# Attention inside a gated decoder block: compressed blocks padded to full tiles, and a head's scaling, transposes and products issued in other steps

## Chip, cores and metric

The program runs on one core of one Trainium2 chip. The metric is device time of one execution in microseconds (us). The engines are named as in the profile: PE is TensorE's matmul side and PEld its weight load, DVE is VectorE, ACT is ScalarE, POOL is GpSimd, SP is the queue that issues most DMAs. Each engine takes its instructions in program order.

## Reference, cut to what matters

One decoder layer in float32 over 256 tokens and 2048 channels. The part that the change touches is the attention of 16 heads of 128 channels in 4 key/value groups. At 256 tokens every selected block is selected and the window covers everything, so a head has three softmaxes over the same queries:

```python
s_c = q . kc          # 15 compressed blocks (padded to 16), masked by block end
s_s = q . k_sel       # 256 keys, causal
s_w = q . k_win       # 256 keys, causal
o = gate0 * softmax(s_c) @ vc + gate1 * softmax(s_s) @ v_sel + gate2 * softmax(s_w) @ v_win
y = sig(gA) * o + sig(gB) * GLU(S5(u))
```

Around it stand large products with weights from HBM: the GLU product `y_s @ w_glu`, the output product, and the MLP.

## The kernel before

All large products are split in two: a weight tile `raw` (128x1024) is rounded on ACT into `hi` (L117), DVE subtracts it into `lo` (L120), and PE multiplies hi by hi, hi by lo and lo by hi (L316, L318, L319). One such tile is a *matmul unit*: 24 matmuls of 256 columns. `run_units` writes out a hand-made order: for each unit it issues the rounding on ACT, then the PE batch of the unit two before it, then the subtraction on DVE, then the steps of background generators that are due. So the instructions of a step stand on DVE behind this unit's `lo`, on ACT behind its `hi`, and on PE behind the batch.

The GLU stage has 32 matmul units, m0 to m31 here. After each of m10 to m25 come two *ada units*, whose second one issues 32 passes with a 32-column weight into the PSUM bank T3 (L1072, about 1.0 us on PE), after which ACT copies 128 columns out of T3 into `s`. Every fourth such pair is followed, after the next batch, by four transposes of `s` into T3 (L1081), which DVE reduces. When a pass of 8 units ends (its last batch runs at m9, m17 and m25), ACT applies four tanh (L1347) and DVE four products ahead of that unit's `lo`.

The attention is a background generator of 34 steps. Its planner gives at matmul unit m5+j, with j from 0 to 25, the steps up to ceil(34*(j+1)/26); nothing is due at ada units. With head h, step 2h is: scores(h) on PE (3 products, banks T0 and T12), the transposes of head h-1 (turn1 into T3, turn2 into A2, with ACT copies to SBUF), and exps(h) (masks and maxima on DVE, six exponentials on ACT). Step 2h+1 is weigh(h) (sums, reciprocal, gates and scaling: nine DVE operations, two ACT copies at L1269) and values(h-1) (five products into A3, L1296 to L1300, and one DVE product). The steps fall so: m5 has 0 and 1, m6 2, m7 3, m8 4 and 5, m9 6, m10 7, m11 8 and 9, m12 10, m13 11, m14 12 and 13, and so on; m25 has 27, m26 28, m27 29 and 30, m28 31, m29 32, m30 33. T0, T12, T3, A2, A3 exist once each: a writer waits until the last reader of the bank's previous use is done. The `hi` and `lo` tiles have three buffers, `P` and `sm` two.

Of the kernel before, what the change touches and what calls it, by code (L numbers as in the profile page):

```python
# [18 lines left out]
NH = 16  # L19
# [12 lines left out]
ATTN_WAIT = 5  # L32
# [49 lines left out]
def block_kernel(ctx, tc, cst_in, x, c, w_ada, b_ada, g_mix, w_in, w_ck2, pe_ck,  # L82
# [3 lines left out]
    nc = tc.nc  # L86
    V, A, PE = nc.vector, nc.scalar, nc.tensor
# [28 lines left out]
    def copy(out, in_, scale=1.0):  # L116
        A.activation(out=out, in_=in_, func=AF.Copy, scale=scale)  # L117
# [19 lines left out]
    ident = cst[:, 0:128]  # L137
# [39 lines left out]
    d_vc = scratch("d_vc", [32, 512])  # L177
# [8 lines left out]
    marks = {}  # L186
# [906 lines left out]
    at = {}  # L1093

    def attn_setup():
        r = region("RX", 16384)
        at["r"] = r
        at["q"] = r[:, 0:4096].rearrange("p (h t) -> p h t", h=16)
        at["v"] = r[:, 4096:6144].rearrange("p (t s n) -> p t s n", t=2, s=2)
        at["K"] = r[:, 6144:8256].rearrange("p (g n) -> p g n", g=4)  # L1100
        at["m"] = r[:, 8256:12352].rearrange("p (h t) -> p h t", h=16)
        at["free"] = r[:, 12352:16384]
        for i, n in enumerate(("tA", "tB")):
            at[n] = region(f"RB{i}", 4096).rearrange("p (h t) -> p h t", h=16)
        nc.sync.dma_start(out=at["K"][:, :, 0:16], in_=d_kc.rearrange("p (g n) -> p g n", g=4))
        vc = cp.tile([128, 512], FT, tag="k0", name="vc")
        nc.sync.dma_start(out=vc[0:32], in_=d_vc)
        at["vc"] = vc.rearrange("p (g n) -> p g n", g=4)
        for g in range(4):
            hs_ = slice(4 * g, 4 * g + 4)  # L1110
            nc.sync.dma_start(out=at["q"][:, hs_, :], in_=d_q[:, hs_, :])
            for s in range(2):
                nc.sync.dma_start(
                    out=at["K"][:, g, 16:528].rearrange("p (t s n) -> p t s n", t=2, s=2)[:, :, s, :],
                    in_=d_k[:, 4 * s + g, :].rearrange("p (t n) -> p t n", t=2))
            yield
            nc.sync.dma_start(out=at["v"][:, :, :, 128 * g:128 * g + 128], in_=d_v[:, :, :, 128 * g:128 * g + 128])
            nc.sync.dma_start(out=at["tA"][:, hs_, :], in_=d_g[:, hs_, :])
            yield
            yield  # L1120
# [91 lines left out]

    def attention():
        fa = at["free"]
        P = [fa[:, 832 * i:832 * i + 832] for i in range(2)]
        PT = [fa[:, 1664:2688]] * 2
        sm = [fa[:, 2688 + 32 * i:2720 + 32 * i] for i in range(2)]
        for i in range(2):
            V.memset(P[i][:, 768:832], 0.0)
        q, K, vv, m = at["q"], at["K"], at["v"], at["m"]  # L1220

        S = {}
# [9 lines left out]
        def exps(h):  # L1232
            S0, S1 = S["s"]
            p, s_ = P[h % 2], sm[h % 2]
            mx, nm, su, mb = s_[:, 0:6], s_[:, 6:12], s_[:, 12:18], s_[:, 18:20]
            pc = p[:, 768:832].rearrange("p (i n) -> p i n", i=2)
            tt(S0[:, 0:272], S0[:, 0:272], m0, OP.add)
            V.tensor_reduce(out=mx[:, 0:1], in_=S0[:, 0:16], axis=AX.X, op=OP.max)
            V.tensor_reduce(out=mx[:, 1:3], in_=S0[:, 16:272].rearrange("p (s n) -> p s n", s=2), axis=AX.X, op=OP.max)
            tt(S1[:, 0, 0:16], S1[:, 0, 0:16], m1c, OP.add)  # L1240
            ts(nm[:, 0:3], mx[:, 0:3], -1.0, OP.mult)
            tt(S1[:, 1, 16:272], S1[:, 1, 16:272], m0[:, 16:272], OP.add)
            V.tensor_reduce(out=mx[:, 3:4], in_=S1[:, 0, 0:16], axis=AX.X, op=OP.max)
            V.tensor_reduce(out=mx[:, 4:6], in_=S1[:, :, 16:272].rearrange("p b (s n) -> p s b n", s=2), axis=AX.XY, op=OP.max)
            ts(nm[:, 3:6], mx[:, 3:6], -1.0, OP.mult)
            A.activation(out=pc[:, 0, 0:16], in_=S0[:, 0:16], func=AF.Exp, bias=nm[:, 0:1])
            for s in range(2):
                A.activation(out=p[:, 128 * s:128 * s + 128], in_=S0[:, 16 + 128 * s:144 + 128 * s], func=AF.Exp,
                             bias=nm[:, 1 + s:2 + s], accum_out=su[:, 1 + s:2 + s])
            A.activation(out=pc[:, 1, 0:16], in_=S1[:, 0, 0:16], func=AF.Exp, bias=nm[:, 3:4])  # L1250
            for s in range(2):
                A.activation(out=p[:, 256 + 256 * s:512 + 256 * s].rearrange("p (b n) -> p b n", b=2),
                             in_=S1[:, :, 16 + 128 * s:144 + 128 * s], func=AF.Exp,
                             bias=nm[:, 4 + s:5 + s], accum_out=su[:, 4 + s:5 + s])

        def weigh(h):
            p, s_ = P[h % 2], sm[h % 2]
            su, cf = s_[:, 12:18], s_[:, 20:26]
            pc = p[:, 768:832].rearrange("p (i n) -> p i n", i=2)
            tt(pc[:, :, 0:16], pc[:, :, 0:16], okm, OP.mult)  # L1260
            V.tensor_reduce(out=su.rearrange("p (i b) -> p i b", i=2)[:, :, 0], in_=pc[:, :, 0:16], axis=AX.X, op=OP.add)
            ts(su, su, 1e-30, OP.max)
            V.reciprocal(out=cf, in_=su)
            tt(cf.rearrange("p (i b) -> p i b", i=2), cf.rearrange("p (i b) -> p i b", i=2),
               gates[:, :, 3 * h:3 * h + 3], OP.mult)
            for i in range(2):
                ts(pc[:, i, 0:16], pc[:, i, 0:16], cf[:, 3 * i:3 * i + 1], OP.mult)
            for s in range(2):
                A.activation(out=p[:, 128 * s:128 * s + 128], in_=p[:, 128 * s:128 * s + 128], func=AF.Copy,  # L1269
                             scale=cf[:, 1 + s:2 + s])  # L1270
                ts(p[:, 256 + 256 * s:512 + 256 * s], p[:, 256 + 256 * s:512 + 256 * s], cf[:, 4 + s:5 + s], OP.mult)

        def turn1(h):
            p, o = P[h % 2], PT[h % 2]
            ps = bank("T3")
            for s in range(2):
                PE.transpose(ps[:, 256 * s:256 * s + 128], p[:, 128 * s:128 * s + 128], ident)
                PE.transpose(ps[:, 256 * s + 128:256 * s + 256], p[:, 256 + 256 * s:384 + 256 * s], ident)
            copy(o[:, 0:512], ps)

        def turn2(h):
            p, o = P[h % 2], PT[h % 2]
            ps = bank("A2")
            for s in range(2):
                PE.transpose(ps[:, 128 * s:128 * s + 128], p[:, 384 + 256 * s:512 + 256 * s], ident)
            for i in range(2):
                PE.transpose(ps[0:32, 256 + 128 * i:384 + 128 * i], p[:, 768 + 32 * i:800 + 32 * i], ident)
            copy(o[:, 512:768], ps[:, 0:256])
            copy(o[0:32, 768:1024], ps[0:32, 256:512])

        def values(h):
            g = h // 4
            o = PT[h % 2]
            ps = bank("A3")
            hd = slice(128 * g, 128 * g + 128)
            PE.matmul(out=ps[:, 0:256], lhsT=vv[:, 0, 0, hd], rhs=o[:, 0:256], start=True, stop=False, skip_group_check=True)  # L1296
            PE.matmul(out=ps[:, 0:256], lhsT=vv[:, 0, 1, hd], rhs=o[:, 256:512], start=False, stop=False, skip_group_check=True)
            PE.matmul(out=ps[:, 0:256], lhsT=at["vc"][0:32, g, :], rhs=o[0:32, 768:1024], start=False, stop=False, skip_group_check=True)
            PE.matmul(out=ps[:, 128:256], lhsT=vv[:, 1, 0, hd], rhs=o[:, 512:640], start=False, stop=False, skip_group_check=True)
            PE.matmul(out=ps[:, 128:256], lhsT=vv[:, 1, 1, hd], rhs=o[:, 640:768], start=False, stop=True, skip_group_check=True)  # L1300
            stt(m[:, h, :], at["tA"][:, h, :], 1.0, ps[:, 0:256], OP.add, OP.mult)

        for h in range(NH + 1):
            if h < NH:
                scores(h)
            if h:
                turn1(h - 1)
                turn2(h - 1)
            if h < NH:
                exps(h)  # L1310
            yield
            if h < NH:
                weigh(h)
            if h:
                values(h - 1)
            yield


# [320 lines left out]
    with tc.manual_schedule():  # L1639
# [39 lines left out]
        def at_(name, f, nxt):  # L1679
# [18 lines left out]
            dict(name="load", gen=attn_setup(), start=marks["glu"] + AS0, end=marks["glu"] + AS1, total=13),  # L1698
            dict(name="tb", gen=load_tb(), start=marks["glu"] + TB0, end=marks["glu"] + TB1, total=4, tick=True),
            dict(name="ht", gen=h_tokens(), start=marks["down"] + 6, end=marks["down"] + 46, total=8),  # L1700
            dict(name="attn", gen=attention(), start=marks["glu"] + ATTN_WAIT, end=marks["out"] - 2, total=34),
        ]
        run_units(bgs)

# [46 lines left out]
```

## Time and profile before

| what | value |
|---|---|
| runs shown | 1748.01 us median of 3 (1745.74 to 1749.41) |
| profiled execution | 1746.7 us, of which 1744.9 us are the span of the profile |
| granted clock, mean over the span | 0.989 |
| PE, DVE, ACT busy over the span | 96%, 67%, 49% |
| attention, first scores to last values | 719.14 to 891.52 us from the span's start |

The profile shows one execution. Busy shares are averages over stages; what the change can be worth is read from the stretch of the attention alone. A group in brackets at a row's end is the idle time of that engine just ahead of it and what ended it.

### The profile page before, as it was taken

What the parts mean: (1) busy time and instruction counts of PE and PEld (TensorE: products, weight loads), DVE (VectorE), ACT (ScalarE), POOL (GpSimd) and SP (SyncE); (2) the same over time, 40 slices, a digit from 0 to 9 for tenths busy, and PEclk for the clock granted to TensorE, in tenths of its full rate; (3) what the DMA queues carried; (4) which work ended last, traced back from release to release, by engine and by line L of the source; (5) the groups of instructions that cost most, each with busy time, mean ns of one, the idle gap of its engine ahead of it and who ended that gap; (6) DMA issues with size and microseconds to landing.
All of it is one profiled execution on the core that took longest, in us unless ns stands there. A gap on an engine that the chain in (4) does not pass through costs nothing.

```text
span 1744.9 us, 31373 instructions
## 1 busy us (share of the span) xinstructions
PE 1682.4 (96%) x12478; PEld 1443.4 (83%) x12478; DVE 1166.3 (67%) x2168; ACT 858.8 (49%) x1424; POOL 30.6 (2%) x53
## 2 busy tenths in 40 slices
PE   6999999889999999999999999999999999999997
PEld 4788899778888877878889999888888888887885
DVE  4868567438898987666656676666666655566555
ACT  3443443564444468655554454444444455555554
POOL 1000000210000000000000000000000000000000
PEclk8999999999999999999999999999999999999999
DMA  8988755948878867966658747777777565655662
GB/s 329 347 274 313 257 182 193 295 137 298 301 266 283 255 220 249 307 233 224 212 184 293 261 156 231 232 241 238 241 249 237 191 189 188 192 190 186 193 194 91
DMA packets 148691, 407.97 MB, mean 234 GB/s; under 512 B 13936, under 2 KB 18512, under 8 KB 147520
## 3 DMA queue, kind: packets, MB, share of 16 engines
q1 hardware_dynamic: 141680, 386.54, 67.3%
q0 software_dynamic: 2032, 10.72, 1.7%
q10 hardware_dynamic: 4832, 8.70, 1.4%
q8 instruction: 98, 1.61, 0.4%
q14 instruction: 49, 0.40, 0.1%
HBM read 386.93 MB, written 16.88 MB: 231 GB/s over the span
## 4 chain that ended last, share of the span: by engine, by line
PE 84%; DVE 7%; ACT 5%; DMA 2%; issue 1%; SPq 0%; ACTq 0%; DVEq 0%
PE A L344 21%; PE A L345 11%; PE A L316 7%; PE A L1615 6%; PE A L318 6%; PE A L1613 6%; PE A L1614 6%; PE A L319 6%; DVE lo L120 3%; PE T L1072 2%; PE T L368 2%; ACT hi L117 1%; ACT RX L117 1%; DMA raw<-in_l_ada_dram 1%; DMA d_c<-RX 1%
## 5 line engine op out<-in xcount | busy, mean ns | idle before, releaser
L120 DVE TENSOR_TENSOR lo<-raw,hi 128x1024 fp32r<-128x1024 f32 (+1 forms) x497 | 605.4, 1222 | 387.0 <-ACT hi L117 377.5
L117 ACT ACTIVATE hi<-raw 128x1024 fp32r<-128x1024 f32 (+1 forms) x497 | 523.8, 1057 | 524.9 <-PE A L344 230.2
L344 PE MATMUL A<-RU,hi 128*128 128x512 f32 x1664 | 592.3, 400 | 1.4 <-DVE st L120 1.3
L345 PE MATMUL A<-RU,lo 128*128 128x256 f32 x1664 | 466.6, 280 | 0.0
L344 PEld LDWEIGHTS A<-RU,hi 128*128 128x128 f32 x1664 | 312.9, 188 | 82.8 <-issue 6.5
L345 PEld LDWEIGHTS A<-RU,lo 128*128 128x128 f32 x1664 | 314.8, 189 | 1.1 <-issue 1.0
L316 PE MATMUL A<-RU,hi 128*128 128x256 f32 x896 | 263.7, 294 | 2.9 <-ACT RU L411 1.5
L319 PE MATMUL A<-RU,lo 128*128 128x256 f32 x896 | 255.6, 285 | 0.5 <-DVE lo L120 0.5
L318 PE MATMUL A<-RU,hi 128*128 128x256 f32 x896 | 255.6, 285 | 0.0
L1615 PE MATMUL A<-lo,RB 128*128 128x512 f32 x512 | 199.7, 390 | 1.4 <-DVE lo L120 1.4
L1613 PE MATMUL A<-hi,RB 128*128 128x512 f32 x512 | 200.2, 391 | 0.8 <-ACT hi L117 0.8
L1614 PE MATMUL A<-hi,RB 128*128 128x512 f32 x512 | 199.2, 389 | 0.0
L316 PEld LDWEIGHTS A<-RU,hi 128*128 128x128 f32 x896 | 173.6, 194 | 19.4 <-issue 13.1
L319 PEld LDWEIGHTS A<-RU,lo 128*128 128x128 f32 x896 | 173.6, 194 | 0.9 <-DVE lo L120 0.8
L318 PEld LDWEIGHTS A<-RU,hi 128*128 128x128 f32 x896 | 173.9, 194 | 0.3 <-DVE RU L129 0.2
L1615 PEld LDWEIGHTS A<-lo,RB 128*128 128x128 f32 x512 | 96.1, 188 | 22.9 <-DVE lo L120 2.7
L1613 PEld LDWEIGHTS A<-hi,RB 128*128 128x128 f32 x512 | 96.1, 188 | 21.0 <-ACT hi L117 1.4
L1614 PEld LDWEIGHTS A<-hi,RB 128*128 128x128 f32 x512 | 96.1, 188 | 19.5
L117 ACT ACTIVATE RB<-RX 128x256 fp32r<-128x256 f32 x160 | 64.1, 402 | 27.4 <-DVE RX L129 27.4
L316 PE MATMUL A<-RB,hi 128*128 128x256 f32 x256 | 73.6, 287 | 1.4 <-ACT RB L117 1.2
L318 PE MATMUL A<-RB,hi 128*128 128x256 f32 x256 | 72.7, 284 | 0.2
L319 PE MATMUL A<-RB,lo 128*128 128x256 f32 x256 | 72.3, 283 | 0.0
(257 smaller groups left out, 1773.2 us busy)
## 6 DMA issues: line engine op xcount, KB each, us to landing
raw<-in_l_ada_dram SPq DMA_DIRECT2D x144, 512.0 KB, 4.9
raw<-in_w_in_dram SPq DMA_DIRECT2D x144, 512.0 KB, 5.0
raw<-in_w_up_dram SPq DMA_DIRECT2D x128, 512.0 KB, 4.1
raw<-in_w_down_dram SPq DMA_DIRECT2D x128, 512.0 KB, 4.6
raw<-in_w_ada_dram SPq DMA_DIRECT2D x48, 512.0 KB, 4.0
raw<-in_w_glu_dram SPq DMA_DIRECT2D x32, 512.0 KB, 5.5
raw<-in_w_out_dram SPq DMA_DIRECT2D x32, 512.0 KB, 6.0
raw<-in_l_keys_dram SPq DMA_DIRECT2D x16, 512.0 KB, 4.7
```

What stands on the lines that cost most here:

```text
L117: A.activation(out=out, in_=in_, func=AF.Copy, scale=scale)
L120: V.tensor_tensor(out=out, in0=a, in1=b, op=op)
L316: PE.matmul(out=o, lhsT=w.hi[:, at], rhs=xh, start=first and j % 2 == 0, stop=False, skip_group_check=True)
L318: PE.matmul(out=o, lhsT=w.hi[:, at], rhs=xl, start=False, stop=False, skip_group_check=True)
L319: PE.matmul(out=o, lhsT=w.lo[:, at], rhs=xh, start=False, stop=last, skip_group_check=True)
L344: PE.matmul(out=o, lhsT=u.hi[:, at], rhs=xp, start=k0 + t == 0, stop=False, skip_group_check=True)
L345: PE.matmul(out=o[:, 0:256], lhsT=u.lo[:, at], rhs=xp[:, 0], start=False, stop=k0 + t == 15, skip_group_check=True)
L368: PE.matmul(out=ps[q:q + 32, :], lhsT=cond[:, t0 + t:t0 + t + 1].to_broadcast([128, 32]), rhs=r[:, t, :], start=t0 == 0, stop=t0 == 12, ti ...
L1072: PE.matmul(out=ps[q:q + 32, 0:128], lhsT=cond[:, kt:kt + 1].to_broadcast([128, 32]), rhs=r[:, kt % 8, :], start=kt < 4, stop=kt >= 12, ti ...
L1613: PE.matmul(out=o, lhsT=xh, rhs=w.hi[:, at_], start=k == 0, stop=False)
L1614: PE.matmul(out=o, lhsT=xl, rhs=w.hi[:, at_], start=False, stop=False)
L1615: PE.matmul(out=o, lhsT=xh, rhs=w.lo[:, at_], start=False, stop=k == 63)
```

## The change

The tile `vc` of compressed values is zeroed by POOL and loaded twice, at partitions 0 to 31 and 96 to 127. The compressed probabilities of the two query halves lie 128 columns apart in zeroed padding, so that both are transposed as 128x128 tiles (the second from column 800 on, whose last 32 columns hold the block), and the product with `vc` contracts over 128 rows in place of 32. The two ACT copies out of A2 become one of 128x512. In the order, weigh(h-1) moves into step 2h, between scores(h) and exps(h); the transposes of head h-1 move to step 2h+1, behind values(h-2), which comes two steps later than before. The generator has 36 steps.

```diff
@@ attn_setup
         vc = cp.tile([128, 512], FT, tag="k0", name="vc")
-        nc.sync.dma_start(out=vc[0:32], in_=d_vc)
+        nc.gpsimd.memset(vc, 0.0)
+        for i in range(2):
+            nc.sync.dma_start(out=vc[96 * i:96 * i + 32], in_=d_vc)
@@ attention
-        P = [fa[:, 832 * i:832 * i + 832] for i in range(2)]
-        PT = [fa[:, 1664:2688]] * 2
+        P = [fa[:, 928 * i:928 * i + 928] for i in range(2)]
+        pcs = [p[:, 768:928].rearrange("p (i n) -> p i n", n=32)[:, ::4] for p in P]
+        o = fa[:, 1856:2880]
-            V.memset(P[i][:, 768:832], 0.0)
+            V.memset(P[i][:, 768:928], 0.0)
...
-            pc = p[:, 768:832].rearrange("p (i n) -> p i n", i=2)
+            pc = pcs[h % 2]
...
-                PE.transpose(ps[0:32, 256 + 128 * i:384 + 128 * i], p[:, 768 + 32 * i:800 + 32 * i], ident)
-            copy(o[:, 512:768], ps[:, 0:256])
-            copy(o[0:32, 768:1024], ps[0:32, 256:512])
+                PE.transpose(ps[:, 256 + 128 * i:384 + 128 * i], p[:, 768 + 32 * i:896 + 32 * i], ident)
+            copy(o[:, 512:1024], ps)
...
-            PE.matmul(out=ps[:, 0:256], lhsT=at["vc"][0:32, g, :], rhs=o[0:32, 768:1024], start=False, stop=False, skip_group_check=True)
+            PE.matmul(out=ps[:, 0:256], lhsT=at["vc"][:, g, :], rhs=o[:, 768:1024], start=False, stop=False, skip_group_check=True)
...
-        for h in range(NH + 1):
+        for h in range(NH + 2):
             if h < NH:
                 scores(h)
-            if h:
-                turn1(h - 1)
-                turn2(h - 1)
+            if 0 < h <= NH:
+                weigh(h - 1)
             if h < NH:
                 exps(h)
             yield
-            if h < NH:
-                weigh(h)
-            if h:
-                values(h - 1)
+            if h > 1:
+                values(h - 2)
+            if 0 < h <= NH:
+                turn(h - 1)
             yield
...
-            dict(name="attn", ..., start=marks["glu"] + ATTN_WAIT, end=marks["out"] - 2, total=34),
+            dict(name="attn", ..., start=marks["glu"] + ATTN_WAIT, end=marks["out"] - 2, total=36),
```

## Rows read from the trace of the kernel before

**Rows 1.** Windows: stretch, length, busy us of PE, PEld, DVE, ACT, POOL, clock, DMA

```profile
719.00:762.00 43.00, 39.70 (x305) 33.25 (x307) 31.79 (x100) 25.21 (x81) 0.00 (x0) 1.00 0.83 285
762.00:858.00 96.00, 93.00 (x963) 78.57 (x955) 59.75 (x196) 50.47 (x164) 0.00 (x0) 1.00 0.67 223
```

**Rows 2.** Timeline of PE and ACT (start, duration, instruction): batch, scores, transposes, copy, ada passes

```profile
784.58 0.38 PE L316 MATMUL A<-RU,hi 128*128 128x256 f32 x1
...
787.55 0.62 PE L1227 MATMUL T<-RX 128*128 128x272 f32 x2
...
788.90 0.27 PE L1277 MATMUL T<-cst,RX 128*128 128x128 f32 x1
...
789.33 0.38 PE L1285 MATMUL A<-cst,RX 128*128 128x128 f32 x2
789.53 0.60 ACT L117 ACTIVATE RX<-T 128x512 f32<-128x512 f32 x1 [3.39 <-PE T L1278]
790.18 1.08 PE L1072 MATMUL T<-raw,cond 128*32 128x128 f32 x32 [0.25 <-ACT RX L117]
```

**Rows 3.** Waits of the weight loads, 705 to 905 us: total, times, longest

```profile
PEld T L1072 <- ACT RX L117: 4.3, 8, 0.5
```

**Rows 4.** Timeline of PE, the last head's values

```profile
889.91 0.59 PE L1297 MATMUL A<-RX 128*128 128x256 f32 x2
890.43 0.69 PE L1298 MATMUL A<-RX,vc 32*128 32x256 f32 x2
891.06 0.49 PE L1299 MATMUL A<-RX 128*128 128x128 f32 x2
891.38 0.39 PE L1300 MATMUL A<-RX 128*128 128x128 f32 x2
891.52 0.36 PE L316 MATMUL A<-RU,hi 128*128 128x256 f32 x1
```

**Rows 5.** Timeline of PE, a head's last transposes and the batch behind

```profile
877.64 0.38 PE L1287 MATMUL A<-cst,RX 128*32 128x128 f32 x2
877.77 0.36 PE L316 MATMUL A<-RU,hi 128*128 128x256 f32 x1
```

**Rows 6.** Timeline of SP and POOL: the vc load, a memset

```profile
710.52 0.61 SPq L1107 DMA_DIRECT2D vc<-d_vc  x1
154.46 0.95 POOL L724 MEMSET s<- 128x1024 f32 x1 [43.90 <-DVE RX L120]
```

**Rows 7.** Timeline of DVE: weigh starts, next operation, start of another head's exps

```profile
735.02 0.18 DVE L120 TENSOR_TENSOR RX<-RX,cst 128x32 f32<-128x32 f32 x1
736.90 0.41 DVE L129 SCALAR_TENSOR_TENSOR RX<-RB,A 128x256 f32<-128x256 f32 x1
749.66 0.44 DVE L120 TENSOR_TENSOR T<-T,cst 128x272 f32<-128x272 f32 x1
```

**Rows 8.** Timeline of ACT and DVE: the hi behind exps and its lo, twice

```profile
731.81 1.06 ACT L117 ACTIVATE hi<-raw 128x1024 fp32r<-128x1024 f32 x1
733.89 1.22 DVE L120 TENSOR_TENSOR lo<-raw,hi 128x1024 fp32r<-128x1024 f32 x1
...
753.31 1.06 ACT L117 ACTIVATE hi<-raw 128x1024 fp32r<-128x1024 f32 x1
754.41 1.23 DVE L120 TENSOR_TENSOR lo<-raw,hi 128x1024 fp32r<-128x1024 f32 x1 [2.20 <-ACT hi L117]
```

**Rows 9.** Timeline of ACT and DVE: a pass's tanh, and the lo behind

```profile
745.01 1.55 ACT L1347 ACTIVATE st<-A,hb 128x256 f32<-128x256 f32 x4
748.52 1.22 DVE L120 TENSOR_TENSOR lo<-raw,hi 128x1024 fp32r<-128x1024 f32 x1
```

**Rows 10.** Timeline of PE: first scores, then the batches issued at m12 and m25

```profile
719.14 0.62 PE L1227 MATMUL T<-RX 128*128 128x272 f32 x2
762.36 0.39 PE L316 MATMUL A<-RU,hi 128*128 128x256 f32 x1
857.93 0.38 PE L316 MATMUL A<-RU,hi 128*128 128x256 f32 x1
```

More of the change, by code (lines that the diff above doesn't have):

```diff
@@ L1214, in attention @@
         fa = at["free"]
-        P = [fa[:, 832 * i:832 * i + 832] for i in range(2)]
-        PT = [fa[:, 1664:2688]] * 2
-        sm = [fa[:, 2688 + 32 * i:2720 + 32 * i] for i in range(2)]
+        P = [fa[:, 928 * i:928 * i + 928] for i in range(2)]
+        pcs = [p[:, 768:928].rearrange("p (i n) -> p i n", n=32)[:, ::4] for p in P]
+        o = fa[:, 1856:2880]
+        sm = [fa[:, 2880 + 32 * i:2912 + 32 * i] for i in range(2)]
         for i in range(2):
-            V.memset(P[i][:, 768:832], 0.0)
+            V.memset(P[i][:, 768:928], 0.0)
         q, K, vv, m = at["q"], at["K"], at["v"], at["m"]
@@ L1258, in weigh @@
             su, cf = s_[:, 12:18], s_[:, 20:26]
-            pc = p[:, 768:832].rearrange("p (i n) -> p i n", i=2)
+            pc = pcs[h % 2]
             tt(pc[:, :, 0:16], pc[:, :, 0:16], okm, OP.mult)
@@ L1271, in weigh, with turn @@
                 ts(p[:, 256 + 256 * s:512 + 256 * s], p[:, 256 + 256 * s:512 + 256 * s], cf[:, 4 + s:5 + s], OP.mult)
-        def turn1(h):
-            p, o = P[h % 2], PT[h % 2]
+        def turn(h):
+            p = P[h % 2]
             ps = bank("T3")
@@ L1279, in turn1 @@
             copy(o[:, 0:512], ps)
-        def turn2(h):
-            p, o = P[h % 2], PT[h % 2]
             ps = bank("A2")
@@ L1286, in turn2 @@
             for i in range(2):
-                PE.transpose(ps[0:32, 256 + 128 * i:384 + 128 * i], p[:, 768 + 32 * i:800 + 32 * i], ident)
-            copy(o[:, 512:768], ps[:, 0:256])
-            copy(o[0:32, 768:1024], ps[0:32, 256:512])
+                PE.transpose(ps[:, 256 + 128 * i:384 + 128 * i], p[:, 768 + 32 * i:896 + 32 * i], ident)
+            copy(o[:, 512:1024], ps)
         def values(h):
             g = h // 4
-            o = PT[h % 2]
             ps = bank("A3")
@@ L1700, in block_kernel @@
             dict(name="ht", gen=h_tokens(), start=marks["down"] + 6, end=marks["down"] + 46, total=8),
-            dict(name="attn", gen=attention(), start=marks["glu"] + ATTN_WAIT, end=marks["out"] - 2, total=34),
+            dict(name="attn", gen=attention(), start=marks["glu"] + ATTN_WAIT, end=marks["out"] - 2, total=36),
         ]
```

## The prediction

> **What bounds the kernel now.** I read the page first: PE is busy in 96% of the span, DVE in 67%, ACT in 49%, so time is gained or lost only where PE stands still or its instructions change. The change acts between the first scores and the last values; the windows of that stretch show PE idle for 3.3 us of the first 43 and 3.0 of the next 96 [rows 1], at full clock (1.00, the 2.4 GHz level). DVE and ACT are busy for 74% and 59% of the first window and 62% and 53% of the second: none is full, but each waits for another in turn. Then I read the timeline of PE. A batch takes 2.97 us (784.58 to 787.55), the scores 1.35, the first four transposes 0.43, all eight 0.87. T3 is where PE meets ACT: the T3 transposes end about 789.33, ACT copies the bank from 789.53, and the ada passes, which write T3 next, start at 790.18, 0.41 later than the transposes would have let them [rows 2]. The list of waits counts 8 of these [rows 3].
>
> **The change part by part.**
>
> Padding. The product with 32 rows costs more than its columns: L1297, with as many columns and full rows, should take 0.43, but L1298 starts 0.52 behind it; L1299 starts 0.63 behind L1298; L1300 0.32 behind L1299, where 128 columns should take half of 0.43 [rows 4]. The excess is 0.09+0.20+0.10 = 0.4 us a head, at least the 0.2 of L1299 alone. With full rows I give a head's values 3x0.43+2x0.22 = 1.73 us; over 16 heads 6.4 us (3.2 to 6.4).
>
> The padded transposes move the same 128 columns. The narrow ones show no switch cost: the batch starts 0.13 us behind L1287 [rows 5]. I take nothing, bounds 0 and the 0.4 of the values. The Trainium skill, "TensorEngine Tiling (Array Packing)", section Key Properties, says that changing the tiling mode drains TensorE; L1298 agrees, L1287 does not. By the rule the transposes would gain as much again.
>
> Set-up. POOL zeroes vc: 0.95 us for twice the columns [rows 6], so some 0.5, and it can run as soon as the tile's earlier use is over; SP issues one load more, 0.61 us [rows 6], ahead of the first queries and keys. PE has batches until the first scores; I take nothing, bound 1.1 us if both come late. The wider memset of P and the merged A2 copy: nothing, since no wait hangs on their length (0.5 us each way).
>
> The order. Steps become ceil(36*(j+1)/26): m5 has 0 and 1, m6 2, m7 3 and 4, m8 5, m9 6, m10 7 and 8, m11 9, m12 10 and 11, m13 12, m14 13, m15 14 and 15, m16 16, m17 17, m18 18 and 19, m19 20, m20 21 and 22, m21 23, m22 24, m23 25 and 26, m24 27, m25 28 and 29, m26 30, m27 31, m28 32 and 33, m29 34, m30 35. An even step now puts on DVE, behind this unit's lo, weigh of the last head (1.9 us [rows 7]) and then exps; ACT is free for the next hi 3.65 us after exps starts on DVE (749.66 to 753.31 [rows 7, 8]). Hi to lo is 1.1 us (2.1 in m6 and m7, where the input's own splits stand between), lo 1.15 [rows 7 to 9]. So from one hi to the next over an even step there are 1.1+1.15+1.9+3.65 = 7.8 us. What is queued behind: the T3 copy of a later step on ACT, and with it PE's ada passes. Before, the T3 copy stood ahead of exps; now, where an even and an odd step share a unit, it stands behind.
>
> I follow three stretches by hand.
>
> m5 to m11. Scores 0 at 719.14 [rows 10]; exps 0 starts after its first product, 719.8; ACT free at 723.5. m6: lo from 725.6 to 726.75, weigh 0 to 728.65, exps 1 frees ACT and T12 at 732.3. m7: PE is ready for the transposes of head 0 at 727.8, gets them at 728.65, and its scores 2 wait for T12 until 732.3: about 3.2 us of idle PE. exps 2 ends (lo 734.4, weigh, 3.65) at 741.1. m8 has only hi and the copies on ACT, 2.0 us; m9 then holds a tanh, behind which lo starts 3.5 later [rows 9]: tanh 744.0, lo 747.5, weigh 2 to 750.55, exps 3 to 754.2. PE, ready for the transposes of head 2 at 749.7, does them by 751.4, and scores 4 wait for T12 until 754.2; after hi and the T3 copy its ada passes run from 755.8 to 756.8. exps 4 frees ACT at 762.5, the ada copy frees T3 at 762.7, the transposes of head 3 end at 763.55, the next ada passes at 765.25. There m12's batch starts, against 762.36 before [rows 10]: +2.9 us. The values of head 3, done by then before, are still owed and are counted in the next stretch.
>
> m12 to m24. A unit with an even and an odd step, from the start of the ada passes ahead of it: on DVE and ACT, passes 1.0, copy 0.2, hi to lo 1.1, lo 1.15, weigh 1.9, exps 3.65, in all 9.0; the T3 copy lets the ada passes start 0.65 later, 9.65. On PE: passes 1.0, batch 2.97, scores 1.35, values 1.73, transposes 0.87: 7.9. PE stands still 1.75 us, in m12, m15 and m18 (there 2.3, since a tanh delays DVE in m17): 5.8. Four lone odd steps (m14, m17, m21, m24) wait the 0.41 as before: 1.6. Small waits for T3 0.7. Work: 13 batches 38.6, 13 ada groups 13.1, ada transposes 0.9, nine heads' scores, transposes and values 12.2+7.8+15.6: 88.2. Sum 96.3, against 857.93-762.36 = 95.6 before [rows 10]: +0.7, with the padding's gain inside.
>
> m25 to the last values. m25 holds tanh, weigh 13, exps 14, values 12 and the transposes of head 13. From its batch: tanh 1.8, lo 5.3 to 6.45, weigh to 8.35, ACT free 12.0, ada passes 12.65; PE reaches the transposes at 6.05, does them by 9.3: idle 2.4 and 3.3. In m28 the transposes of the last head wait for its weigh: 0.6. Work: 6 batches 17.8, ada 1.4, 2 scores 2.7, 3 transposes 2.6, 4 values 6.9: 31.4. Sum 37.7 against 891.52-857.93 = 33.6 before [rows 4, 10]: +4.1.
>
> 2.9+0.7+4.1 = 7.7 us. The profiled execution took 1746.7, so 1754.4; behind the attention the output product goes on without idle PE at its start [rows 4], so nothing is given back. The profiled execution lies 1.3 below the median of the runs; against that median the forecast is +6.4 us, 0.37%. About 0.2% (3.5 us) is what a measurement of this kernel can tell from no change.
>
> **The rivals.**
>
> Faster: PE is the last to arrive everywhere. The place is the T3 copy behind exps in m12, m15, m18 and m25: it costs nothing from the point where DVE and ACT need 1.75 us less than the 9.65 above. Then the padding's 6.4 and about half of the 6.3 idle of both windows [rows 1] come off: 1746.7-6.4-3.1 = 1737. For it: ACT idles 3.39 us ahead of its copy [rows 2], so today it runs ahead of PE. Against: that lead is had because exps stands behind the copy.
>
> Same: the narrow transposes drain too, or the start loses nothing. The first gives 16x0.4 = 6.4 more: 1748.0; the second takes off 2.9 to 1751.5 at its edge. Against the first is the 0.13 of L1287. The first is the rule of the Trainium skill's tiling page.
>
> The padding gains nothing, because the price sits in the weight of `vc` and not in its 32 rows: 7.7+6.4 = 14.1, 1761. Against: L1297 and L1299 differ from L1298 in rows alone.
>
> **How the numbers follow.** Forecast 0.52, faster 0.22, same 0.18, padding useless 0.08. The forecast's own range is 1750 to 1759: 1.1 for the set-up, 3.2 for the padding's lower bound upward, and downward some 0.2 for each of the twenty-odd waits in the walk. Eight in ten need both sides: 1738 to 1761 leaves out half of the faster case and half of the worst. Slower by over 0.2%: the forecast less its lower edge, and the worst: 0.57; same 0.20; faster 0.23.
>
> **What would show it.** Right: L1298 0.43 behind L1297 and L1299 0.43 behind L1298; four ada groups (m12, m15, m18, m25) that start over 1.5 us behind their transposes, with ACT's exponentials as what ended last; scores 2 and 4 waiting for ACT; the last values ending about 899. Wrong: ada groups that all wait 0.4, or last values ahead of 891.

## The result and the profile after

The changed kernel takes 1758.82 us (median of 4 runs, 1757.75 to 1760.78) against 1746.88 us before: ratio 1.0066, 95% interval 1.0053 to 1.008. It is slower by 0.66%; the forecast was 0.37%, on the same side, and the time lies in the range of 1738 to 1761. The profiled execution took 1758.04 us with a span of 1756.3.

First the windows of the three stretches of the prediction in the changed kernel, cut where PE starts the first scores, the batches of m12 and m25, and ends the last values (columns as in [rows 1]):

```profile
718.46:764.61 46.15, 41.25 (x303) 35.84 (x301) 31.72 (x101) 26.16 (x82) 0.00 (x0) 0.89 0.75 259
764.61:862.53 97.92, 90.70 (x961) 81.28 (x957) 59.03 (x195) 51.88 (x156) 0.00 (x0) 1.00 0.65 216
862.53:902.15 39.62, 34.07 (x260) 31.86 (x257) 21.20 (x60) 18.50 (x45) 0.56 (x1) 0.91 0.58 192
```

The stretches take 46.15, 97.92 and 39.62 us, where the kernel before took 43.22, 95.57 and 33.59 [rows 4, 10]: +2.93, +2.35, +6.03, in all 11.3. This is the whole difference of the two spans (11.4). PE is idle for 4.9, 7.2 and 5.6 us in them, 17.7 together, where before it was 6.6. And the granted clock is 0.89 and 0.91 in the first and the last, where before it was 1.00 throughout: PE's busy time over the three, 166.0 us, is not below the 165.8 of before, although the padding shortens its products.

What PE waited for between 705 and 910 us, from the list of waits of the changed kernel (total, times, longest):

```profile
PE T L1072 <- ACT RX L117: 11.0, 9, 3.5
PE T L1281 <- ACT RX L1273: 2.7, 3, 1.9
PE T L1231 <- ACT RX L1252: 2.7, 2, 1.3
PE T L1232 <- ACT RX L1256: 1.3, 2, 0.9
```

The first is the ada passes behind the T3 copy (four of 1.69, 1.68, 2.61 and 3.46 us in m12, m15, m18 and m25, and five of 0.31), the second the transposes behind their scaling, the last two the first and second products of scores 2 and 4, behind the exponentials that read T0 and T12. One of the four, in m15, on the timelines of PE and ACT:

```profile
793.20 0.27 ACT L1250 ACTIVATE RX<-T,RX 128x16 f32<-128x16 f32 x1 [1.27 <-DVE RX L124]
794.28 0.38 PE L1289 MATMUL A<-cst,RX 128*128 128x128 f32 x2
795.24 0.47 ACT L1256 ACTIVATE RX<-T,RX 128x256 f32<-128x256 f32 x1
795.69 0.60 ACT L117 ACTIVATE RX<-T 128x512 f32<-128x512 f32 x1
796.35 1.08 PE L1072 MATMUL T<-raw,cond 128*32 128x128 f32 x32 [1.68 <-ACT RX L117]
```

The transposes into T3 are over at about 794, but ACT stands in the exponentials of the next head and gets to the T3 copy at 795.69. Before, the copy began 0.20 us behind the start of L1285 [rows 2]; here L1286 starts at 794.06, and the copy 1.63 later.

The padding did what it should. PE's timeline of a head's last values and of the transposes ahead of a batch:

```profile
837.90 0.59 PE L1297 MATMUL A<-RX 128*128 128x256 f32 x2
838.33 0.59 PE L1298 MATMUL A<-RX,vc 128*128 128x256 f32 x2
838.76 0.38 PE L1299 MATMUL A<-RX 128*128 128x128 f32 x2
838.98 0.39 PE L1300 MATMUL A<-RX 128*128 128x128 f32 x2
839.20 0.27 PE L1281 MATMUL T<-cst,RX 128*128 128x128 f32 x1
...
740.40 0.38 PE L1289 MATMUL A<-cst,RX 128*128 128x128 f32 x2
740.54 0.36 PE L316 MATMUL A<-RU,hi 128*128 128x256 f32 x1
```

From L1297 to L1298 it is 0.43 us in place of 0.52, from L1298 to L1299 0.43 in place of 0.63, from L1299 to L1300 0.22 in place of 0.32 [rows 4]. From the last transposes to the batch it is 0.14, where it was 0.13 [rows 5]: the wide transposes cost nothing and gain nothing. The Trainium skill ("TensorEngine Tiling (Array Packing)", Key Properties) says that a change of tiling mode drains TensorE. The 0.4 us around the product with 32 rows agree with it; the 0.13 and 0.14 us behind the transposes show no such price for 32 columns.

The set-up cost nothing either; POOL and SP in the changed kernel:

```profile
695.77 0.53 POOL L1107 MEMSET vc<- 128x512 f32 x1 [338.22 <-PE T L888]
709.87 1.07 SPq L1109 DMA_DIRECT2D vc<-d_vc  x2
```

The memset is done 13 us ahead of the loads, and the first scores start at 718.46, not later than the 719.14 of before.

### The profile page after: what moved, and what is told of

It is laid out like the page before. It is cut to its first block, busy times and chain, and to the rows that moved or that the text cites. A ratio compares the mean times of both kernels' runs of the same rounds, so it can differ in the third digit from the quotient of the medians.

```text
span 1756.3 us, 31388 instructions
## 1 busy us (share of the span) xinstructions
PE 1683.8 (96%) x12478; PEld 1451.7 (83%) x12478; DVE 1166.0 (66%) x2168; ACT 860.0 (49%) x1408; POOL 31.0 (2%) x54
## 4 chain that ended last, share of the span: by engine, by line
PE 82%; DVE 8%; ACT 5%; DMA 2%; issue 1%; SPq 1%; ACTq 0%; DVEq 0%
PE A L344 21%; PE A L345 11%; PE A L316 7%; PE A L1614 6%; PE A L1613 6%; PE A L1612 6%; PE A L318 6%; PE A L319 6%; DVE lo L120 3%; PE T L1072 2%; PE T L368 1%; ACT hi L117 1%; ACT RX L117 1%; DMA raw<-in_l_ada_dram 1%; DVE RX L124 1%
## 5 line engine op out<-in xcount | busy, mean ns | idle before, releaser
L117 ACT ACTIVATE hi<-raw 128x1024 fp32r<-128x1024 f32 (+1 forms) x497 | 524.0, 1057 | 527.2 <-PE A L344 231.1
L117 ACT ACTIVATE RB<-RX 128x256 fp32r<-128x256 f32 x160 | 64.1, 402 | 27.4 <-DVE RX L129 27.4
```

## The experiments

Ratios are to the kernel before, timed on the same chip; a difference of two versions in us is one of medians, and where they were timed apart it is good to 1 or 2 us. PE's time from the first scores to the last values is 172.4 us before and 183.7 in the changed kernel.

**The two halves apart.** Padding alone is the changed kernel with the old loop and 34 steps; order alone is the kernel before with the new loop and 36 steps. The loop of padding alone against the changed kernel:

```diff
-        for h in range(NH + 2):
+        for h in range(NH + 1):
...
-            if 0 < h <= NH:
-                weigh(h - 1)
+            if h:
+                turn(h - 1)
             if h < NH:
                 exps(h)
             yield
-            if h > 1:
-                values(h - 2)
-            if 0 < h <= NH:
-                turn(h - 1)
+            if h < NH:
+                weigh(h)
+            if h:
+                values(h - 1)
```

> The changed kernel's padding (zeroed vc at two places, full transposes, one copy out of A2, 128-row product) with the order and the 34 steps of the kernel before. Theory (the order costs, the padding gains): L1298 and L1299 each start 0.43 us behind the product ahead of them, 0.4 us a head; of these 6.4 us 4 to 6.4 show, since some heads at the start wait for ACT anyway: 0.25 to 0.4% faster than the kernel before. Rival (the padding gains nothing or costs, and is part of the loss): within 0.1% of the kernel before or slower.

Measured: 1743.93 us, ratio 0.9981 (0.9969 to 0.9993). Faster, by a little less than expected: PE's time over the attention falls by 3.6 us (168.8). The three stretches take 43.15, 92.83 and 32.81 us, so the middle shows most of the saving (2.74) and the start none (0.07):

```profile
721.90:765.05 43.15, 39.72 (x313) 35.22 (x311) 31.68 (x100) 25.05 (x77) 0.00 (x0) 0.96 0.85 282
```

There the transposes wait 2.03 us for their scaling where it was 1.37 before, and the granted clock is 0.96: what the padding saves there is lost again.

> The order and the 36 steps of the changed kernel with the unpadded blocks of the kernel before. Theory: the whole loss and more sits here; 4 to 6.4 us slower than the changed kernel, that is 0.9 to 1.05% slower than the kernel before, with the same three stretches of low clock. Rival (the loss comes from the padded tiles): no slower than the changed kernel, 0.66% or less over the kernel before.

Measured: 1763.99 us, ratio 1.0104 (1.0086 to 1.0122). The loss is the order's, 1.0%; the padding gives back about 0.4% of it. The rival is out.

**The T3 wait taken away.** The ada passes that follow an even and an odd step in one unit go to bank T0:

```diff
-            ps = bank("T3")
+            ps = bank(at.get("ada", "T3"))
...
             if h < NH:
                 exps(h)
+            at["unit"], at["ada"] = now[0], "T3"
             yield
...
+            at["ada"] = "T0" if at.get("unit") == now[0] else "T3"
             yield
```

> The changed kernel, with the ada passes that follow a unit with an even and an odd step (m12, m15, m18, m25) written into bank T0 in place of T3, so that they need not wait for the T3 copy behind exps; all else equal. T0 is free once the first three exponentials are done, some 1.5 to 2 us ahead of the T3 copy. Theory (the T3 copy behind exps sets PE's waits): the four waits of 1.69, 1.68, 2.61 and 3.46 us shrink to under 0.5 in the first three and by about 2 in m25, and the low clock behind m25 goes: 6 to 10 us faster than the changed kernel, 0.1 to 0.3% over the kernel before. Rival (ACT and DVE are the bound, PE only shows it): the waits come back at the next transposes or scores, and the time stays within 2 us of the changed kernel.

Measured: 1751.12 us, ratio 1.0027 (1.0016 to 1.0038), 7.7 us less than the changed kernel. The ada waits by what ended them (L117 is the T3 copy, L1252 the exponentials that read T0):

```profile
PE T L1072 <- ACT RX L117: 2.3, 5, 1.1
PE T L1072 <- ACT RX L1252: 1.8, 2, 1.3
```

The waits of m12 and m15 are gone, those of m18 and m25 are 0.5 and 1.3, and the granted clock behind m25 is 1.00. A wait of 1.1 us in m17 is new. The T3 copy behind exps, with the low clock that its waits bring in m25, is worth about six tenths of the loss (7.7 of 11.9 us by the medians, 6.8 by the ratios).

**Other units for the same steps.**

```diff
-            dict(name="attn", ..., total=36),
+            dict(name="attn", ..., total=35),
```

> The changed kernel with total=35 in place of 36, so that the steps fall on other units: behind m5 an even step never shares a unit with the odd step after it, all doubled units hold an odd step and then an even one; the last step is issued in m30 too. Theory: no T3 copy stands behind exps of its own unit, so the waits of m12, m15, m18 and m25 (9.4 us) fall to 0.3 each and the low clock of m25 goes; the waits of scores 2 and 4 for T12 in m7 and m10 stay: 8 to 11 us faster than the changed kernel, within 0.2% of the kernel before. Rival (the work put between two hi tiles, weigh and exps together, is what costs, in whatever unit): less than 3 us faster than the changed kernel.

Measured: 1752.65 us, ratio 1.0033 (1.002 to 1.0046): 6.2 us less, below the expected 8 to 11. The four waits did fall to 0.3 or less, but one came up that I had not followed. PE in m26 of this run:

```profile
868.02 0.28 PE L319 MATMUL A<-RU,lo 128*128 128x256 f32 x1
871.86 1.12 PE L1081 MATMUL T<-cst,s 128*128 128x128 f32 x4 [3.56 <-ACT s L117]
```

m25 now holds steps 27 and 28, and the copy of the ada tile `s` stands on ACT behind exps 14, which stands behind weigh 13 and the tanh. The ada transposes wait 3.56 us for it.

**Exps ahead of weigh.** On top of total=35, and then with 36 steps:

```diff
-            if 0 < h <= NH:
-                weigh(h - 1)
             if h < NH:
                 exps(h)
+            if 0 < h <= NH:
+                weigh(h - 1)
             yield
```

> The kernel of the run before (the changed kernel with total=35), and in an even step exps(h) ahead of weigh(h-1) in place of behind it. Theory: the bank T12 and the ACT queue come free 1.9 us earlier in every even step, so the waits of scores 2 and 4 (1.3 and 0.9 us each, with the low clock behind them) and the 3.6 us wait of the ada transposes in m26 shrink; the transposes of head 0 and 2 in m7 and m10 wait a little longer for their weigh: 3 to 6 us faster than with total=35 alone, 1746.5 to 1750. Rival (the sum of weigh and exps counts, not their order): within 1.5 us of it.

Measured: 1743.5 us, ratio 0.9976 (0.9965 to 0.9987): some 9 us less than with weigh first, more than the theory's 3 to 6, and faster than the kernel before. PE no longer waits in scores, but it waits 3.2 and 1.8 us for the scaling of heads 0 and 2. The attention with weigh first and with exps first:

```profile
720.26:897.31 177.05, 166.23 (x1514) 148.56 (x1513) 111.80 (x355) 96.12 (x283) 0.57 (x1) 0.95 0.68 229
716.89:883.75 166.86, 157.85 (x1515) 143.24 (x1513) 112.78 (x355) 94.80 (x283) 0.56 (x1) 1.00 0.72 243
```

Of the 10.2 us between them only 1.8 are idle time (10.8 and 9.0); the rest is PE's busy time on the same matmuls, at a mean granted clock of 0.95 and of 1.00. How much of it the order brings by itself, and how much what the clock did in these two executions, is not shown.

> The changed kernel with exps(h) ahead of weigh(h-1) and the 36 steps left as they are: the fourth corner beside the changed kernel (36, weigh first), total=35 with weigh first, and total=35 with exps first. Theory (both count: where the steps meet in a unit, and how long T12, T3 and ACT stay taken): the waits of scores 2 and 4 go, but in m12, m15, m18 and m25 the transposes now wait for weigh, which ends at about the same time as before, so those four waits stay near 1.5 to 3 us: 1751 to 1756. Rival (the order of weigh and exps is all): 1743 to 1747, as with total=35.

Measured: 1755.79 us, ratio 1.0043 (1.0029 to 1.0057). As the theory has it: the four waits stay, at another instruction. The transposes now wait for weigh:

```profile
PE T L1281 <- ACT RX L1273: 14.0, 6, 4.5
PE T L1072 <- ACT RX L117: 2.5, 8, 0.3
```

So with 36 steps either order loses. Both count, and each counts for more with the other: from 36 to 35 steps the ratios fall by 5.8 us with weigh first and by 11.7 with exps first, and exps first gains 4.0 us with 36 steps and 10.0 with 35.

**The scaling moved alone.** Padding and 34 steps, an even step of scores(h), weigh(h-1), the transposes of head h-1 and exps(h), and the odd step of values(h-1). Against padding alone:

```diff
             if h:
+                weigh(h - 1)
                 turn(h - 1)
             if h < NH:
                 exps(h)
             yield
-            if h < NH:
-                weigh(h)
             if h:
                 values(h - 1)
```

> Padding and 34 steps, and only the scaling moved: an even step is scores(h), weigh(h-1), transposes of head h-1, exps(h); the odd step has values(h-1) alone. The T3 copy stands ahead of exps on ACT, as in the kernel before. Theory (the T3 copy behind exps is what costs): waits for T3 stay at 0.4 us, the start still has 7.8 us from hi to hi, PE waits up to 1 us more for some transposes: 1744 to 1749, at most 0.1% over the kernel before. Rival (weigh ahead of exps on DVE is what costs, wherever the transposes stand): 1754 or more.

Measured: 1758.89 us, ratio 1.0058 (1.0045 to 1.0071). My expectation was wrong by ten us, and the rival's number came. The waits of this run:

```profile
PE T L1281 <- ACT RX L1273: 15.1, 10, 3.6
PE T L1072 <- ACT RX L117: 1.7, 7, 0.3
PE A L1296 <- ACT RX L117: 0.7, 3, 0.2
```

The ada passes wait 0.3 each, as expected: the T3 copy ahead of exps does take that wait away. But the transposes, in the same step as their scaling, wait 3.5 to 3.6 us in m6, m9 and m17, and 0.6 in most other even steps. The rival's reason is not the one that shows (no PE instruction waits long for exponentials); weigh at the front of an even step costs PE in each of the placements tried: through T3 when the transposes come a step later in the same unit, directly when they come at once.

**The products a head later, alone.** Padding, the old loop, `values(h - 2)` in place of `values(h - 1)`, and two buffers of transposed probabilities. Against padding alone, cut:

```diff
-        o = fa[:, 1856:2880]
+        O = [fa[:, 1856 + 1024 * i:2880 + 1024 * i] for i in range(2)]
...
-        for h in range(NH + 1):
+        for h in range(NH + 2):
...
-            if h:
-                values(h - 1)
+            if h > 1:
+                values(h - 2)
```

> Padding alone, order of the kernel before, and only the products a head later: values(h-2) in place of values(h-1), with two buffers for the transposed probabilities; 34 steps planned, the last two issued in m30. Theory: the products' place is harmless, their waits for the A2 copy go (three of 0.3 to 0.6 us): 0 to 1.5 us faster than padding alone. Rival (later products are part of the loss, since they pile up at the end): more than 2 us slower than padding alone.

Measured: 1745.85 us, ratio 0.9986 (0.9978 to 0.9995), against 0.9981 with padding alone; the intervals overlap. Later products neither help nor hurt as far as this can tell; a loss of over 2 us is not seen.

**The low clock.** The changed kernel with transposes of the identity, read by nobody, where PE waits in m7 and m25:

```diff
+        def fill(tag, n):
+            ps = bank(tag)
+            for i in range(n):
+                PE.transpose(ps[:, 0:128], ident, ident)
...
+            if h in (0, 13):
+                fill(*{0: ("A3", 6), 13: ("A2", 16)}[h])
...
             copy(o[:, 512:1024], ps)
+            if h in (0, 13):
+                fill(*{0: ("A3", 14), 13: ("A0", 28)}[h])
```

> The changed kernel (36 steps) with transposes of the identity that nobody reads put in where PE waits in m7 (6 ahead of and 14 behind the transposes of head 0, into A3) and in m25 (16 ahead of and 28 behind those of head 13, into A2 and A0): some 0.11 us each. Theory (the clock falls because PE stood still shortly before): the batch in m26 takes 3.0 in place of 4.3 us, the ada passes of m25 1.0 in place of 1.9, the batch in m8 3.0 in place of 4.5; 2 to 4 us faster than the changed kernel, since DVE and ACT set part of the start anyway. Rival (the clock falls for another reason, or it costs nothing because the queues behind set the pace): no faster, or slower by what the fillers take beyond the waits, 0 to 2 us.

Measured: 1759.18 us, ratio 1.0063 (1.0049 to 1.0078): no gain that the timing can tell. The windows show the effect itself. First the changed kernel in m25 and m26: values and the wait for weigh, transposes, the wait for T3, ada passes, batch with its wait (the eighth number is the granted clock):

```profile
866.85:870.62 3.77, 1.90 (x11) 1.55 (x9) 3.56 (x11) 0.45 (x2) 0.00 (x0) 1.00 0.36 117
870.62:871.66 1.04, 1.04 (x8) 0.93 (x8) 1.01 (x5) 0.24 (x1) 0.00 (x0) 1.00 0.91 291
871.66:875.29 3.63, 0.17 (x3) 0.01 (x1) 2.06 (x8) 2.70 (x12) 0.00 (x0) 0.73 0.15 54
875.29:877.15 1.86, 1.86 (x32) 1.39 (x32) 0.00 (x0) 0.43 (x1) 0.00 (x0) 0.50 0.00 0
877.15:881.44 4.29, 4.29 (x28) 4.29 (x25) 1.23 (x1) 1.22 (x2) 0.00 (x0) 0.65 0.84 263
```

And the same place with the fillers: the second wait, ada passes, batch:

```profile
869.76:873.38 3.62, 3.22 (x31) 2.98 (x29) 2.05 (x8) 2.70 (x12) 0.00 (x0) 1.00 0.14 53
873.38:874.39 1.01, 1.01 (x33) 0.81 (x33) 0.00 (x0) 0.43 (x1) 0.00 (x0) 1.00 0.00 0
874.39:877.36 2.97, 2.97 (x29) 2.97 (x25) 1.23 (x1) 1.23 (x2) 0.00 (x0) 1.00 0.75 163
```

The waits are as long (3.62 and 3.63 us), PE is busy in them, the clock stays at 1.00, and passes and batch take 1.01 and 2.97 in place of 1.86 and 4.29: 2.2 us. From m25's batch to the last values PE takes 37.5 us in place of 39.6. In m8 the batch also falls, from 4.55 to 3.06, but the batch issued in m10 then waits 1.5 us for the tanh, and the first stretch takes 46.10 in place of 46.15: there DVE and ACT set the pace and the low clock was free. So idle time of PE does bring the clock down here, at a price of about 2 us of the 11.3 in m25 and m26; that the total fell by those 2 us is seen in the profiled execution (1755.63 us, the fastest of six) and not by the median. In all the low clock lengthens PE's work in the changed kernel by an estimated 7 to 8 us: its matmuls take 166.0 us of busy time, and 157.9 at a clock of 1.00 in total=35 with exps first. Most of that lies at the start, where the fillers took it away in m7 and m8 without gain.

**The best version.** total=35, exps first, and the last ada transposes one unit later:

```diff
-                defer(1, fin)
+                defer(2 if now[0] == marks["out"] - 7 else 1, fin)
```

> total=35 with exps first, and the last set of ada transposes put off by one unit (from m26 to m27), so that it doesn't wait for the copy of its tile, which stands behind m25's exponentials on ACT. Theory: the 2.1 us wait in m26 goes and nothing else changes: 1.5 to 2.2 us faster than the run with total=35 and exps first, 0.3 to 0.4% faster than the kernel before. Rival (the wait moves to the next instruction that needs ACT): the same as that run within 0.5 us.

Measured: 1741.79 us, ratio 0.9962 (0.9949 to 0.9976): the fastest of all, and the wait of the ada transposes is gone from its list; what is left above 0.4 us are the two waits for weigh at the start:

```profile
PE T L1281 <- ACT RX L1273: 4.8, 2, 3.2
PE T L1072 <- ACT RX L117: 1.6, 5, 0.3
```

The interval overlaps that of total=35 with exps first (0.9965 to 0.9987), so the last step's own share is only likely. It overlaps that of padding alone (0.9969 to 0.9993) too: that any version of the new order beats padding alone is not shown.

> total=35 with exps first, with the unpadded blocks of the kernel before. Theory (the padding is worth 0.4 us a head wherever PE sets the pace): 4.5 to 6.4 us slower than the padded run with the same order, so within 0.15% of the kernel before; the order by itself then neither gains nor loses. Rival (with this order ACT sets the pace and the padding is hidden): less than 2 us slower than the padded run.

Measured: 1747.75 us, ratio 1.0001 (0.999 to 1.0011), 4.3 us over the padded run with this order, just under the 4.5 to 6.4 that were expected. With these units and exps first the new order is worth nothing by itself that the timing can tell, and the padding makes the gain.

## Why the prediction was right, and where it was off

*The side and its mechanism.* Right. The T3 copy behind exps in m12, m15, m18 and m25 was named with a wait of 1.75 us in the first two and 2.3 and 3.3 in the others; the trace has 1.69, 1.68, 2.61 and 3.46. The T0 run shows that these waits, with the low clock behind them, are the larger part of the loss, since the time falls by 7.7 us when they shrink; total=35 takes them away by other means and gains 6.2, with a new wait of 3.56 in m26.

*The size.* Too small. The walk has +7.7 us, the profile shows +11.3 and the medians +11.9. The forecast of +6.4 is smaller still, because 1.3 us were taken off for the distance of one profiled execution from the median of three runs. That distance belongs to the execution and not to the change; with four runs the median before is 1746.88, 0.2 us from the profiled execution. Without that subtraction the forecast is 0.44%.

*The start, +2.9.* Measured +2.93. The second products of scores 2 and 4 start at 731.88 and 753.82, when ACT frees T12 (in the walk 732.3 and 754.2), and the ada passes of m10 at 755.86 (755.8). PE's part was another than in the walk: it had no low clock, which stretches m8's batch from 2.97 us to 4.55 and these ada passes from 1.01 to 1.68, inside time that the walk has as waiting. The sum held because DVE and ACT set the end of that stretch, as the fillers show. That it agrees to 0.03 us is luck: the first scores came 0.7 us earlier than before, and the walk's wait of 1.2 us for T3 in m11 did not come.

*The middle, +0.7.* Measured +2.35; the term was too small by 1.65. I had counted two sets of ada transposes where three run (0.44 us each), and had given the ada passes no price behind full products: behind scores they start 1.44 to 1.45 us after the scores' start in place of 1.35, six times. The rest is the waits themselves, some 0.06 to 0.5 longer each than in the walk, in all 0.95; of the 0.7 allowed for small waits 0.3 did not come.

*The end, +4.1.* Measured +6.03; the term was too small by 1.9. Waits and work were right: with the fillers, which keep the clock up, the stretch takes 37.45 us against the walk's 37.7. What was missing is the low clock behind the two long waits of m25, 0.85 us on the ada passes and 1.32 on the batch.

*The padding, 0.4 us a head.* Right in PE's own spacing. What shows of 6.4 us depends on the order around it: by the ratios about 6.6 under the new order with 36 steps (1.0104 against 1.0066), 4.4 with 35 and exps first, 3.3 under the old one, each good to 2 us or so. The rival that it gains nothing is out.

*Nothing for set-up and wide transposes.* Right, by the rows above.

*The rivals.* Faster failed at the point that was named for it: DVE and ACT need the 9.65 us from one ada group to the next (786.55 to 796.35 in m15 is 9.80), and PE stands there. The narrow transposes that drain were out by 0.13 against 0.14.

## What to carry to other kernels

When engines run in order and hand work round, a reorder is priced by writing down, for each unit, what is ahead of the hand-over on each queue: here 1.9 us of scaling and a head's exponentials, put ahead of a PSUM copy, delayed it, and with it an unrelated product that used the same bank. Which steps meet in a unit and the order inside a step act together (36 or 35 steps: 5.8 us with one order, 11.7 with the other), so the number of steps of a planner is to be tried with the order, not after it. A version that gains in one part and loses in another is worth taking apart: the padding by itself beat both kernels, and with 35 steps and exps first it carried the new order too, which by itself gained nothing.

## What the runs showed of the hardware that was not expected

PE's granted clock fell to 0.50 (1.2 GHz, of the two levels 1.2 and 2.4) behind some of PE's waits. In the changed kernel it did so in m7 behind waits of 0.61 and 1.34 us, in m10 behind 1.34 and 0.91, and in m25 behind 1.88 and 3.46; behind the single waits of 1.69 us in m12 and 2.61 in m18 it stayed at 1.00. A rule on the length or the spacing of waits does not come out of the runs. With the order alone a single wait of 2.21 us in m18 was followed by 0.50. And behind the same single wait of 3.19 us for the scaling of head 0 the clock was 1.00 in the profile of total=35 with exps first and 0.50 in that of the best version. Head 0's transposes in these two, then the ada passes of m18 with the order alone and in the changed kernel (the eighth number is the clock):

```profile
728.71:729.70 0.99, 0.99 (x8) 0.90 (x9) 0.25 (x1) 0.99 (x2) 0.00 (x0) 1.00 1.10 355
732.27:734.00 1.73, 1.73 (x8) 1.73 (x9) 0.46 (x2) 1.73 (x5) 0.00 (x0) 0.50 1.06 353
821.01:822.90 1.89, 1.89 (x33) 1.41 (x33) 0.00 (x0) 0.44 (x2) 0.00 (x0) 0.50 0.00 0
820.00:821.00 1.00, 1.00 (x32) 0.81 (x32) 0.00 (x0) 0.43 (x1) 0.00 (x0) 1.00 0.00 0
```

So a wait can cost more than its length, and one profile does not tell whether it will. The Trainium skill ("TensorE: Matmul & The Clock Gate", Part 1) tells that the array's clock is released by recent activity; the fillers in m25 agree, with 1.00 in place of 0.50.

The ada passes start about 0.1 us later behind full products than another product would. In the kernel before they start 0.32 us behind the last product of the values, whose columns take 0.22; in the changed kernel 0.52 us behind the last product of the scores in place of 0.43:

```profile
750.75 0.39 PE L1300 MATMUL A<-RX 128*128 128x128 f32 x2
751.07 1.08 PE L1072 MATMUL T<-raw,cond 128*32 128x128 f32 x32
...
778.29 0.59 PE L1233 MATMUL T<-RX 128*128 128x256 f32 x2
778.81 1.08 PE L1072 MATMUL T<-raw,cond 128*32 128x128 f32 x32
...
877.42 0.38 PE L1285 MATMUL A<-cst,RX 128*128 128x128 f32 x2
```

The 32 columns of their weight alone are not the reason: in the last row, of the kernel before, the 32-column transposes of [rows 5] follow full ones after 0.22 us, no later than full ones do. What the 0.1 us is made of stays open.
